# An inner seven-product scheme in one block product of the SwiGLU pairs

## The chip, the cores and the metric

The kernel runs on one core of one Trainium2 chip. The metric is the device time of one execution in microseconds. TensorE (PE) multiplies, with weight loads (PEld) that overlap matmuls; VectorE (DVE), ScalarE (ACT) and GpSimd (POOL) compute on vectors; SyncE (SP) and ScalarE issue DMAs. PSUM has eight banks of 128 x 512 float32, which TensorE writes and VectorE and ScalarE read.

## The reference, cut to what matters

One layer over 1024 positions and 1024 channels, all in float32: a modulated RMSNorm, a mixer (gated DeltaNet and short convolution) and its output projection, a second modulated norm, SwiGLU, and a final norm. The change lies in the SwiGLU:

```python
def swiglu(h, w_gate, w_up, w_down):
    return (jax.nn.silu(h @ w_gate) * (h @ w_up)) @ w_down
```

Here `h` is 1024 x 1024, `w_gate` and `w_up` are 1024 x 2816 (22 column tiles of 128), and `w_down` is 2816 x 1024.

## The kernel before, in words

**Precision.** A float32 operand is split into a high part (`hi`, rounded to float32r by ScalarE: `cast`, `split`) and a low part (the rest, subtracted by VectorE: `low`). A product takes three matmuls: hi x hi, hi x lo, lo x hi.

**Pairs and steps.** The products `h @ w_gate` and `h @ w_up` go over eleven pairs of column tiles (`p` = 0 to 10). For a pair, weights and `h` are cut into 2 x 2 blocks (by column tile and by half of the 1024 channels; by half of the channels and by half of the positions), and seven block products take the place of eight. `STEPS` names them in order: a PSUM bank pair (X, Y or Z), a weight block or sum of blocks (A11, A12, S2, S1, S3, S4, A22) and a block or sum of `h` (B11, B21, T2, T1, T3, B22, T4). `run(p, s)` issues step `s`: for gate (`q` = 0) and up (`q` = 1), four channel tiles `k` with three matmuls of 512 columns each, 24 in all. Step 1 is Y = A12 x B21. X collects four steps, Z two; in between, ScalarE copies X or Z out (`keep`), and VectorE adds what comes later (`close`). SiLU (`silu`, ScalarE) and the product with the up half (`act`, VectorE) follow.

**What sets the order.** In this stage no scheduler moves anything: each engine runs its instructions in the order in which the code issues them. `block(p, s)`, issued behind `run(p, s)`, holds what VectorE and ScalarE do beside the next steps: closing sums, weight sums of the pair (`sum_n`), casts and lows for later steps, those of A11 and A12 for the next pair (in blocks 5 and 6), the sums of the finished blocks that the down projection needs, and at `s == 0` the SiLU of bank X of the pair before and its product. DMAs wait in a list (`store`) until `flush` puts them on SP's queue; the weights of the next pair are loaded there at steps 3 and 5, into a buffer whose old blocks must have been read.

**Banks and buffers.** Bank X of pair p and Y of pair p + 1 are the same two banks (`bk`), so step 1 of a pair can write only when the SiLU and the product on X of the pair before have read. Split weights lie in eight buffers (`slot`): four in the ring `hl` and four under the tag `gl`; pair 0 uses `hl` alone.

**Ahead of the pairs.** While TensorE does the last tiles of the output projection (`w_out_tile`), the normed positions are transposed into `H[k]` (`first_half`): `H[0]` to `H[3]` hold B11 and `H[4]` to `H[7]` B21, each a split tile of 128 channels x 512 positions. `sums_x` makes the sums T1 to T4 by position.

Lines: the recording layer issues everything ahead of this stage from line 450, TensorE issues here from line 88, the others from line 89.

## Time and profile before

| | |
|---|---|
| time, median of 3 runs (lowest, highest) | 1170.82 us (1170.2, 1170.95) |
| the profiled execution: time, span | 1169.63 us, 1167.8 us |
| granted TensorE clock | 0.999 |
| TensorE busy | 1157.2 us (99%) |
| weight loads busy | 968.1 us (83%) |
| VectorE, ScalarE busy | 920.7 us (79%), 546.1 us (47%) |
| matmuls | 5582, each with a weight load |
| pair 0 begins, pair 1 begins, the pairs end | 522.9, 570.6, 951.4 us |

Times in rows are microseconds from the start of the span. A row of a timeline gives start, duration, engine, line, operation, tiles (written <- read) and count, and in brackets the idle time ahead of it with what ended it. A row of a group gives busy time and mean duration in ns, then the idle time ahead. The end of a matmul is modelled, so the price of one is read from the distance of starts. PE's busy time counts matmuls that wait in the pipeline.

### The profile page before, as it was taken

To read this page: it belongs to the slowest core of one execution; us is meant where nothing else is said; L and a number is where in the kernel's file an instruction comes from. 1 tells how busy PE (TensorE), PEld (TensorE's weight loads), DVE (VectorE), ACT (ScalarE), POOL (GpSimd) and SP (SyncE) were. 2 spreads that over 40 slices of the span, in tenths; PEclk is the share of its full clock that TensorE was granted. 3 is DMA by queue.
4 is the path that set the end of the run, shared out by engine and by line. 5 is a ranking of instruction groups with operands and counts; after the bars stand their busy time and mean duration, and the time that the engine had idled before them with its cause. 6 is when DMAs were issued, how large, how long until landed. Compare 5 with 4: busy or idle time off the path is not lost.

```text
span 1167.8 us, 16456 instructions
## 1 busy us (share of the span) xinstructions
PE 1157.2 (99%) x5582; PEld 968.1 (83%) x5582; DVE 920.7 (79%) x1702; ACT 546.1 (47%) x1182; POOL 59.6 (5%) x100
## 2 busy tenths in 40 slices
PE   9999999999999999999999999999999999999997
PEld 7888888888888888888888888888888888888886
DVE  7898988898987898669776777776777687788676
ACT  6779733458634552325433333333333365443343
POOL 1110101001101010200000000000000000000002
PEclk9999999999999999999999999999999999999999
DMA  9633455534325555434264456446554589869413
GB/s 363 246 99 110 118 171 163 168 114 137 113 66 163 163 193 175 174 101 144 80 216 158 140 201 223 159 132 222 191 184 137 194 306 393 308 203 340 144 37 145
DMA packets 126453, 207.06 MB, mean 177 GB/s; under 512 B 20513, under 2 KB 45089, under 8 KB 126369
## 3 DMA queue, kind: packets, MB, share of 16 engines
q1 hardware_dynamic: 121520, 202.86, 51.5%
q10 hardware_dynamic: 4848, 3.15, 0.9%
q8 instruction: 44, 0.72, 0.3%
q14 instruction: 41, 0.33, 0.1%
HBM read 150.91 MB, written 55.05 MB: 176 GB/s over the span
## 4 chain that ended last, share of the span: by engine, by line
PE 93%; DVE 3%; ACT 2%; DMA 1%; issue 1%; SPq 0%; ACTq 0%; DVEq 0%
PE acc L88 35%; PE acc L450 24%; PE dn L88 17%; PE o L88 4%; PE o L450 4%; PE A L450 1%; PE K L450 1%; DMA wr<-in_w_in_dram 1%; DVE xo L89 1%; PE ab L450 1%; PE w L450 1%; PE u L450 1%; PE O L450 1%; PE tr L450 1%; PE kk L450 1%
## 5 line engine op out<-in xcount | busy, mean ns | idle before, releaser
L450 PE MATMUL acc<-h,u 128*128 128x512 f32 x1200 | 301.0, 398 | 0.0
L450 PEld LDWEIGHTS acc<-h,u 128*128 128x128 f32 x1200 | 219.0, 188 | 41.1
L88 PE MATMUL acc<-h,hl 128*128 128x512 f32 x600 | 140.1, 390 | 0.0
L88 PEld LDWEIGHTS acc<-h,hl 128*128 128x128 f32 x600 | 112.4, 188 | 23.2
L88 PE MATMUL acc<-h,u 128*128 128x512 f32 x456 | 106.1, 389 | 0.0
L88 PE MATMUL acc<-T,hl 128*128 128x512 f32 x432 | 101.4, 390 | 0.4 <-ACT cc L89 0.4
L88 PEld LDWEIGHTS acc<-h,u 128*128 128x128 f32 x456 | 85.6, 188 | 17.7
L88 PEld LDWEIGHTS acc<-T,hl 128*128 128x128 f32 x432 | 80.9, 188 | 17.5 <-ACT cc L89 0.9
L88 PE MATMUL dn<-h,h 128*128 128x512 f32 x396 | 90.7, 389 | 0.0
L89 DVE TENSOR_TENSOR xo<-xo,dn 128x512 f32<-128x512 f32 x84 | 57.0, 683 | 42.3 <-PE dn L88 34.8
L89 ACT COPY cc<-acc 128x512 f32<-128x512 f32 x66 | 38.4, 590 | 108.3 <-PE acc L88 108.3
L88 PEld LDWEIGHTS dn<-h,h 128*128 128x128 f32 x396 | 74.3, 188 | 15.4
L88 PE MATMUL acc<-T,u 128*128 128x512 f32 x360 | 84.0, 389 | 0.0
L88 PEld LDWEIGHTS acc<-T,u 128*128 128x128 f32 x360 | 67.6, 188 | 14.0
L450 ACT CAST u<-raw 128x512 fp32r<-128x512 f32 x69 | 42.7, 622 | 66.0 <-PE acc L450 64.3
L89 DVE TENSOR_TENSOR cc<-cc,acc 128x512 f32<-128x512 f32 x66 | 43.8, 682 | 29.8 <-PE acc L88 29.8
L89 DVE TENSOR_TENSOR hl<-R,hl 128x512 fp32r<-128x512 f32 x60 | 39.4, 687 | 33.5 <-ACT hl L89 33.4
L450 DVE TENSOR_TENSOR u<-raw,u 128x512 fp32r<-128x512 f32 x82 | 56.0, 685 | 11.9 <-ACT u L450 11.7
L450 DVE SCALAR_TENSOR_TENSOR cv<-pr,cols_a,cv 128x512 f32<-128x512 f32 x72 | 52.9, 745 | 0.1
L89 ACT CAST h<-rw 128x512 fp32r<-128x512 f32 x57 | 32.7, 618 | 40.5 <-PE dn L88 34.6
L89 ACT CAST hl<-R 128x512 fp32r<-128x512 f32 x60 | 35.7, 622 | 23.5 <-DVE R L89 10.7
L89 DVE TENSOR_TENSOR u<-R,u 128x512 fp32r<-128x512 f32 x46 | 30.1, 686 | 20.6 <-ACT u L89 20.5
(343 smaller groups left out, 1993.2 us busy)
## 6 DMA issues: line engine op xcount, KB each, us to landing
raw<-in_w_in_dram SPq DMA_DIRECT2D x82, 256.0 KB, 3.1
am_scr<-cc SPq DMA_DIRECT2D x77, 256.0 KB, 4.6
raw<-in_w_ada_dram SPq DMA_DIRECT2D x56, 256.0 KB, 3.4
rw<-am_scr SPq DMA_DIRECT2D x55, 256.0 KB, 5.2
rw<-bm_scr SPq DMA_DIRECT2D x53, 256.0 KB, 5.3
bm_scr<-raw SPq DMA_DIRECT2D x51, 256.0 KB, 5.4
R<-in_w_gate_dram SPq DMA_DIRECT2D x22, 512.0 KB, 4.3
R<-in_w_up_dram SPq DMA_DIRECT2D x22, 512.0 KB, 5.5
```

What stands on the lines that cost most here:

```text
L88: return call(*a, **k)
L89: ins = call(*a, **k)
L450: ins = call(*a, **k)
```

## The change

Step 1 of pairs 1 to 10 is itself computed by seven products instead of eight. A12 (128 gate columns and 128 up columns, 512 channels) is cut by gate and up and by halves of the channels; B21 by halves of the channels and of the positions. Each of the products m1 to m7 has two channel tiles of three matmuls with 256 columns: 42 matmuls in place of 24 with 512.

The weight side needs three sums of blocks, in four operands of VectorE: `inner_sums` (four sums of 256 columns), and split weights I0 to I3 (`inner_cast`, `inner_low`: three of 512 columns and one of 256, where A12 had two of 512). The side of `h` needs q1, q2 and q3, made once in `inner_half`, which takes the place of `first_half(range(4, 8))`, and a fourth sum, which `inner_last` writes over the second half of `H[4]` and `H[5]` behind step 6 of pair 0. Pair 0 keeps the old step 1.

The seven products share two banks: x (m1, m6, m7, m4) in the bank that the SiLU frees, y (m2) and z (m5, m3) in the two halves of the other. Between products that add to one bank, ScalarE copies the sum so far (K0 behind m1, K2 behind m5, K1 behind m6, K3 behind m7), and `close_inner` adds copies and banks. m7 and m4 stand behind the two halves of step 2. The copy of X (`keep`) is issued ahead of the inner products, and in block 0 the product on X and its store stand ahead of S1 and S2. The scratch space for DMA descriptors is set to 1024 bytes.

```diff
+    def inner_half(a):
+        DVE.tensor_tensor(db3[:, a:a + 1], b2c[:, 6 + a:7 + a], b2c[:, 4 + a:5 + a], ALU.subtract)
+        bank = {}
+        for k in (4 + a, 6 + a):
+            bank[k] = allb.get("tr")
+            H[k][0] = tr_split(lambda: h_slot(k, 0), [x2n[i][:, k * P:(k + 1) * P] for i in range(4)], bank[k], b2c[:, k:k + 1])
+        pa, pb = bank[4 + a], bank[6 + a]
...
+        DVE.tensor_copy(f3, pa[:, HN:HT])
+        DVE.tensor_tensor(f1, f3, pa[:, 0:HN], ALU.subtract)
+        DVE.tensor_tensor(f2, pb[:, HN:HT], f1, ALU.subtract)
+        DVE.tensor_tensor(f3, pb[:, HN:HT], f3, ALU.subtract)
+        for n, f, col in (("q1", f1, None), ("q2", f2, b2c[:, 6 + a:7 + a]), ("q3", f3, db3[:, a:a + 1])):
+            hi, lo = tq[n][:, 0, a, :], tq[n][:, 1, a, :]
+            if col is None:
+                split(f, hi, lo, DVE)
+            else:
+                ACT.activation(hi, f, AF.Identity, bias=col, scale=1.0)
+                DVE.scalar_tensor_tensor(lo, f, col, hi.bitcast(F32), ALU.add, ALU.subtract)
+
+    def inner_last():
+        for a in (0, 1):
+            t = raw_t([P, 2, HN])
+            DVE.tensor_tensor(t, H[6 + a][0][:, :, 0:HN].bitcast(F32), tq["q2"][:, :, a, :].bitcast(F32), ALU.subtract)
+            DVE.tensor_tensor(t[:, 0], t[:, 0], t[:, 1], ALU.add)
+            q4 = H[4 + a][0][:, :, HN:HT]
+            split(t[:, 0], q4[:, 0], q4[:, 1], DVE)
...
-    first_half(range(4, 8))
+    inner_half(0)
+    inner_half(1)
...
+        def inner_sums(self):
+            g, u = self.m["A12"]
...
+            DVE.tensor_tensor(L[:, 0], u[:, 0:2], u[:, 2:4], ALU.add)
+            DVE.tensor_tensor(L[:, 1], L[:, 0], g[:, 0:2], ALU.subtract)
+            DVE.tensor_tensor(L[:, 3], g[:, 0:2], u[:, 0:2], ALU.subtract)
+            DVE.tensor_tensor(L[:, 2], g[:, 2:4], L[:, 1], ALU.subtract)
+            Lf = L.rearrange("p s k c -> p (s k) c")
+            self.iu = [None] * 4
+            self.src = [g, Lf[:, 0:4], Lf[:, 4:8], u[:, 2:4]]
...
-        n = n_slot[0] - 14
+        n = n_slot[0] - 12
...
+    INNER = {"m1": (0, 0, "x"), "m2": (0, 2, "y"), "m5": (1, 0, "z"), "m6": (1, 2, "x"), "m3": (2, 0, "z"), "m7": (2, 2, "x"), "m4": (3, 2, "x")}
...
+    def inner(p, ms):
...
+        for m in ms:
+            i, k0, d = INNER[m]
+            first = m in ("m1", "m2", "m5")
+            u = W[p].iu[i]
+            for k in range(2):
+                for n, (wi, xi) in enumerate(((0, 0), (0, 1), (1, 0))):
+                    pmm(iw[p][d], u[:, wi, k0 + k, :], inner_b(m, k, xi), first and k == 0 and n == 0, k == 1 and n == 2, not first)
+            if m in ("m1", "m5", "m6", "m7"):
...
+                ACT.copy(ik[p][:, {"m1": 0, "m6": 1, "m5": 2, "m7": 3}[m]], iw[p][d])
+
+    def close_inner(p, n):
+        (g, u), K, w = c[p][n], ik[p], iw[p]
+        DVE.tensor_tensor(g, g, flat(K[:, 0:2]), ALU.add)
+        DVE.tensor_tensor(u[:, HN:HT], u[:, HN:HT], K[:, 2], ALU.add)
+        DVE.tensor_tensor(g, g, w["yz"], ALU.add)
+        DVE.tensor_tensor(u[:, HN:HT], u[:, HN:HT], K[:, 3], ALU.add)
+        DVE.tensor_tensor(u[:, 0:HN], u[:, 0:HN], w["x"], ALU.add)
...
         elif s == 2:
-            close(p, "p1", "Y")
+            close_inner(p, "p1")
...
         elif s == 6:
             close(p, "u2", "Z")
             if n:
-                n.cast("A12", 0)
+                n.inner_sums()
+                n.inner_cast(0)
             silu(p, "u2")
             if n:
-                n.cast("A12", 1)
-                n.low("A12", 0)
-                n.low("A12", 1)
+                n.inner_cast(1)
+                n.inner_low(0)
+                n.inner_low(1)
...
+            if n:
+                for i in (2, 3):
+                    n.inner_cast(i)
+                    n.inner_low(i)
...
+        if s == 6:
+            inner_last()
...
-            run(p, s)
+            if s == 1:
+                keep(p, "p1", "X")
+                inner(p, ("m1", "m2", "m5", "m6", "m3"))
+            elif s == 2:
+                run(p, s, (0,))
+                inner(p, ("m7",))
+                run(p, s, (1,))
+                inner(p, ("m4",))
+            else:
+                run(p, s)
```

What this makes of the order on the engines is shown at three places.

TensorE, step 1 of pair 1 before: `acc_5922` and `acc_5923` are Y of gate and up, the `hl` tiles the split A12, the `h` tiles B21.

```order
L88 MATMUL acc_5922<-h_0_960_5218,hl_5862 128x512 x3
L88 MATMUL acc_5922<-h_0_962_5226,hl_5862 128x512 x3
L88 MATMUL acc_5922<-h_0_964_5234,hl_5862 128x512 x3
L88 MATMUL acc_5922<-h_0_966_5242,hl_5862 128x512 x3
L88 MATMUL acc_5923<-h_0_960_5218,hl_5865 128x512 x3
```

And now, from m1 to the first rows of step 2: `acc_5976` is bank x, `acc_5977` holds y and z, `u_5897`, `u_5900` and `u_5907` are I0, I1 and I2, the `q` tiles are q1 and q2.

```order
L88 MATMUL acc_5976<-h_0_960_5223,u_5897 128x256 x3
L88 MATMUL acc_5976<-h_0_966_5252,u_5897 128x256 x3
L88 MATMUL acc_5977<-h_0_962_5231,u_5897 128x256 x3
L88 MATMUL acc_5977<-h_0_968_5260,u_5897 128x256 x3
L88 MATMUL acc_5977<-q_5087,u_5900 128x256 x6
L88 MATMUL acc_5976<-q_5088,u_5900 128x256 x6
L88 MATMUL acc_5977<-h_0_962_5231,u_5907 128x256 x3
L88 MATMUL acc_5977<-h_0_968_5260,u_5907 128x256 x3
L88 MATMUL acc_5934<-T_1008_5536,hl_5966 128x512 x3
```

One wide product has become five narrow ones ahead of step 2; m6 returns to the bank of m1, and m3 to the bank of m5.

ScalarE between pair 0 and the first steps of pair 1, before: `cc_5787<-acc_5451` is the SiLU on bank X of pair 0, `S_5912` is S2, `acc_5883` and `acc_5884` are X of pair 1 and `S_5910` is S1.

```order
L89 ACTIVATE cc_5748<-cc_5748 128x512
L89 CAST hl_5865<-R_5745 128x512
L89 ACTIVATE cc_5787<-acc_5451 128x512
L89 CAST u_5914<-S_5912 128x512
L89 CAST u_5916<-S_5912 128x512
L89 COPY cc_5948<-acc_5883 128x512
L89 COPY cc_5948<-acc_5884 128x512
L89 CAST u_5951<-S_5910 128x512
```

The same place now; `L_5892` are the sums of `inner_sums`, `raw_5913` and `raw_5918` those of `inner_last`, `L_5984` the copies K.

```order
L89 ACTIVATE cc_5778<-cc_5778 128x512
L89 CAST u_5900<-L_5892 128x512
L89 CAST u_5907<-L_5892 128x512
L89 CAST u_5910<-R_5775 128x256
L89 CAST h_0_960_5223<-raw_5913 128x256
L89 CAST h_0_966_5252<-raw_5918 128x256
L89 ACTIVATE cc_5817<-acc_5481 128x512
L89 CAST hl_5966<-S_5964 128x512
L89 CAST hl_5968<-S_5964 128x512
L89 COPY cc_5973<-acc_5934 128x512
L89 COPY cc_5973<-acc_5935 128x512
L89 COPY L_5984<-acc_5976 128x256
```

The SiLU on X now stands behind the casts of `inner_last`, and the first copy K0 behind the casts of S2 and the copies of X.

VectorE from the first of the two sums behind the product of pair 0 (`cc_5526`) to the sum S1 (`S_5962`), now; before, these two sums were followed at once by S1.

```order
L89 TENSOR_TENSOR cc_5526<-cc_5778,cc_5817 128x512
L89 TENSOR_TENSOR cc_5778<-cc_5525,cc_5778 128x512
L89 TENSOR_TENSOR u_5907<-L_5892,u_5907 128x512
L89 TENSOR_TENSOR u_5910<-R_5775,u_5910 128x256
L89 TENSOR_TENSOR raw_5913<-h_0_962_5231,q_5088 128x512
L89 TENSOR_TENSOR raw_5913<-raw_5913 128x256
L89 TENSOR_TENSOR h_0_960_5223<-raw_5913,h_0_960_5223 128x256
L89 TENSOR_TENSOR raw_5918<-h_0_968_5260,q_5088 128x512
L89 TENSOR_TENSOR raw_5918<-raw_5918 128x256
L89 TENSOR_TENSOR h_0_966_5252<-raw_5918,h_0_966_5252 128x256
L89 TENSOR_TENSOR cc_5817<-acc_5482,cc_5817 128x512
L89 TENSOR_TENSOR S_5962<-R_5772,R_5775 128x1024
```

Two lows, six instructions of `inner_last` and the product on X have come in ahead of S1.

More of the change, by code (lines that the diff above doesn't have):

```diff
@@ L546 @@
     db2 = cst.tile([P, 4], F32, name="db2", tag="db2")
+    db3 = cst.tile([P, 2], F32, name="db3", tag="db3")
     su = []
@@ L1558, in first_half @@
             H[k][0] = tr_split(lambda: h_slot(k, 0), [x2n[i][:, k * P:(k + 1) * P] for i in range(4)], allb.get("tr"), b2c[:, k:k + 1])
+    HN = HT // 2
+    tq = {n: hp_.tile([P, 2, 2, HN], F32R, name=n, tag=n) for n in ("q1", "q2", "q3")}
+    def inner_half(a):
[5 more added lines that the diff above has]
+        pa, pb = bank[4 + a], bank[6 + a]
+        f12, f3 = raw_t(), raw_t()
+        f1, f2, f3 = f12[:, 0:HN], f12[:, HN:HT], f3[:, 0:HN]
+        DVE.tensor_copy(f3, pa[:, HN:HT])
[16 more added lines that the diff above has]
+            split(t[:, 0], q4[:, 0], q4[:, 1], DVE)
     def w_out_tile(t, ch):
@@ L1690, in mat, with inner_cast, inner_low @@
                 self.low(n, q)
+        def inner_sums(self):
+            g, u = self.m["A12"]
+            L = self.L = mp.tile([P, 4, 2, P], F32, name=nm("L"), tag="L", bufs=1)
+            DVE.tensor_tensor(L[:, 0], u[:, 0:2], u[:, 2:4], ALU.add)
[5 more added lines that the diff above has]
+            self.src = [g, Lf[:, 0:4], Lf[:, 4:8], u[:, 2:4]]
+        def inner_cast(self, i):
+            u = self.iu[i] = slot()
+            ACT.copy(u[:, 0] if i < 3 else u[:, 0, 2:4], self.src[i])
+        def inner_low(self, i):
+            u = self.iu[i]
+            hi, lo = (u[:, 0], u[:, 1]) if i < 3 else (u[:, 0, 2:4], u[:, 1, 2:4])
+            DVE.tensor_tensor(lo, self.src[i], hi.bitcast(F32), ALU.subtract)
     n_slot = [0]
@@ L1734, in run, with inner_b @@
                     pmm(ps, u[:, wi, k, :], x_[:, xi, :], first and k == 0 and n == 0, k == 3 and n == 2, not first)
+    iw, ik = {}, {}
+    INNER = {"m1": (0, 0, "x"), "m2": (0, 2, "y"), "m5": (1, 0, "z"), "m6": (1, 2, "x"), "m3": (2, 0, "z"), "m7": (2, 2, "x"), "m4": (3, 2, "x")}
+    def inner_b(m, k, xi):
+        if m in ("m1", "m4"):
+            return H[4 + k][0][:, xi, 0:HN] if m == "m1" else H[4 + k][0][:, xi, HN:HT]
+        if m in ("m2", "m3"):
+            return H[6 + k][0][:, xi, 0:HN] if m == "m2" else H[6 + k][0][:, xi, HN:HT]
+        return tq[{"m5": "q1", "m6": "q2", "m7": "q3"}[m]][:, xi, k, :]
+    def inner(p, ms):
+        if p not in iw:
+            x_, yz = bank_tile(bk[p][0]["Y"], "acc"), bank_tile(bk[p][1]["Y"], "acc")
+            iw[p] = dict(yz=yz, y=yz[:, 0:HN], z=yz[:, HN:HT], x=x_[:, 0:HN])
+        for m in ms:
[6 more added lines that the diff above has]
+            if m in ("m1", "m5", "m6", "m7"):
+                if p not in ik:
+                    ik[p] = mp.tile([P, 4, HN], F32, name=nm("L"), tag="L", bufs=1)
+                ACT.copy(ik[p][:, {"m1": 0, "m6": 1, "m5": 2, "m7": 3}[m]], iw[p][d])
[6 more added lines that the diff above has]
+        DVE.tensor_tensor(u[:, 0:HN], u[:, 0:HN], w["x"], ALU.add)
     def cc(p, n):
@@ L1800, in block @@
                 o = p - 1
-                ACT.activation(c[o]["z5"][1], bk[o][0]["X"], AF.Silu)
+                a12 = c[o]["z5"][1]
+                ACT.activation(a12, bk[o][0]["X"], AF.Silu)
+                DVE.tensor_tensor(a12, bk[o][1]["X"], a12, ALU.mult)
+                store(o, "A12", a12)
             if w:
@@ L1806, in block @@
                     w.cast("S2", q)
-            if p > 0:
-                a12 = c[o]["z5"][1]
-                DVE.tensor_tensor(a12, bk[o][1]["X"], a12, ALU.mult)
-                store(o, "A12", a12)
             if w:
@@ L1815, in block @@
             if w:
-                keep(p, "p1", "X")
+                if not p:
+                    keep(p, "p1", "X")
                 w.cast("S1", 0)
@@ L1973 @@
                 flush()
-            run(p, s)
+            if s == 1:
+                keep(p, "p1", "X")
+                inner(p, ("m1", "m2", "m5", "m6", "m3"))
[6 more added lines that the diff above has]
+                run(p, s)
             block(p, s)
@@ L2175 @@
     from concourse.bass_utils import run_bass_kernel_spmd as _run
-    nc = _bacc.Bacc("TRN2", target_bir_lowering=False, num_devices=1)
+    nc = _bacc.Bacc("TRN2", target_bir_lowering=False, num_devices=1, dynamic_dma_scratch_size=1024)
     arrays, args = {}, []
```

## The prediction

> **What bounds the kernel now.** I read the page first, then the waits of TensorE, then its timeline. The page:

> ```profile
> span 1167.8 us, 16456 instructions
> PE 1157.2 (99%) x5582; PEld 968.1 (83%) x5582; DVE 920.7 (79%) x1702; ACT 546.1 (47%) x1182; POOL 59.6 (5%) x100
> ...
> PE 93%; DVE 3%; ACT 2%; DMA 1%; issue 1%; SPq 0%; ACTq 0%; DVEq 0%
> ```

> TensorE is busy for 99% of the span, and 93% of the chain that ended last is its own work. Between 430 and 1000 us the waits of TensorE are one line, and the window of all eleven pairs shows the same:

> ```profile
> PE acc L88 <- ACT cc L89: 0.4, 1, 0.4
> ```

> ```profile
> 523.00:951.00 428.00, 427.56 (x1928) 354.91 (x1927) 313.76 (x464) 161.39 (x290) 0.76 (x2) 1.00 0.51 173
> ```

> In 428.00 us TensorE is idle for 0.44 us, at the full granted clock (1.00). So in the pairs a matmul saved is time saved, and every wait that the change brings to TensorE is time lost; nothing absorbs it. VectorE and ScalarE are off the path while their results come early enough. The timeline of TensorE gives the price of a wide matmul (512 columns):

> ```profile
> 570.63 11.04 PE L88 MATMUL acc<-h,hl 128*128 128x512 f32 x48
> 581.51 5.60 PE L88 MATMUL acc<-T,u 128*128 128x512 f32 x24
> ...
> 646.79 11.04 PE L88 MATMUL acc<-h,u 128*128 128x512 f32 x48
> ```

> Steps 0 and 1 of pair 1 run from 570.63 to 581.51, 48 matmuls in 10.88 us: 0.2267 us each, 5.44 us a step. Step 0 of pair 3 begins at 646.79.

> **The price of a narrow matmul.** The change puts 42 matmuls of 256 columns in the place of 24 of 512, each with its own weight load as before. No row has 256 columns. The nearest below:

> ```profile
> 239.77 1.06 PE L450 MATMUL K<-A,kt 128*128 128x128 f32 x8
> 240.58 0.70 PE L450 MATMUL acc<-h,u 128*128 128x512 f32 x2
> 241.12 1.05 PE L450 MATMUL O<-A,at 128*128 128x128 f32 x8
> ```

> From 239.77 to 241.12 stand eight matmuls of 128 columns and two wide ones: (1.35 - 2 x 0.2267) / 8 = 0.112 us. A quarter of the columns costs half the time, so there something else sets the pace, and what both sizes share is one weight load each. So 256 columns cost at least 0.112 us, about half a wide one (0.1133) if the columns set the pace and nothing is fixed, and 0.150 us if a straight line joins the two rows. I take 0.120: both limits that I can name lie at 0.112 to 0.113, and 7 ns are for what of a wide interval doesn't halve with its columns. Then step 1 costs 42 x 0.120 = 5.04 us instead of 5.44: 0.40 us saved in each of ten pairs (0.74 at 0.112; 0.86 lost at 0.150).

> A load's own record is longer than the narrow interval, so loads overlap what runs ahead of them:

> ```profile
> L450 PEld LDWEIGHTS K<-A,kt 128*128 128x128 f32 x120 | 15.5, 191 | 1.9 <-DVE A L450 0.5 <-issue 0.2
> ```

> [...]

> **Rows for the other engines.** Groups by form, busy time and mean ns behind the bar:

> ```profile
> L89 ACT COPY cc<-acc 128x512 f32<-128x512 f32 x66 | 38.4, 590 | 108.3 <-PE acc L88 108.3
> ...
> L89 DVE TENSOR_TENSOR cc<-cc,acc 128x512 f32<-128x512 f32 x66 | 43.8, 682 | 29.8 <-PE acc L88 29.8
> ```

> ```profile
> L450 DVE SCALAR_TENSOR_TENSOR S<-S,egl,K 128x128 f32<-128x128 f32 x56 | 15.7, 340 | 1.3 <-PE K L450 1.2
> L89 DVE TENSOR_TENSOR S<-S,R 128x1024 f32<-128x1024 f32 x10 | 12.2, 1225 | 0.3
> ```

> ```profile
> L450 ACT COPY S<-K x4: 265/279/300, 212.4 to 212.9; 128x128 f32<-128x128 f32 x4
> ```

> So 256 columns cost VectorE between 0.34 and 0.68 us, about 0.42, or some 0.34 in a row of independent ones (wide ones start 0.60 apart), and ScalarE between 0.28 and 0.59, about 0.38.

> **Pair 1: the wait that the change adds.** VectorE and ScalarE between pair 0 and pair 1:

> ```profile
> 567.30 1.28 DVE L89 TENSOR_TENSOR cc<-cc,acc 128x512 f32<-128x512 f32 x2
> 568.81 0.69 DVE L89 TENSOR_TENSOR hl<-R,hl 128x512 fp32r<-128x512 f32 x1 [0.23 <-ACT hl L89]
> 571.53 0.69 DVE L89 TENSOR_TENSOR hl<-R,hl 128x512 fp32r<-128x512 f32 x1 [2.03 <-ACT hl L89]
> ...
> 572.86 1.29 DVE L89 TENSOR_TENSOR cc<-cc,cc 128x512 f32<-128x512 f32 x2
> 574.07 1.22 DVE L89 TENSOR_TENSOR S<-R,R 128x1024 f32<-128x1024 f32 x1
> ...
> 576.46 0.68 DVE L89 TENSOR_TENSOR cc<-acc,cc 128x512 f32<-128x512 f32 x1
> ```

> ```profile
> 571.40 0.59 ACT L89 ACTIVATE cc<-acc 128x512 f32<-128x512 f32 x1
> 576.58 1.14 ACT L89 CAST u<-S 128x512 fp32r<-128x512 f32 x2 [4.58 <-DVE S L89]
> 577.63 1.07 ACT L89 COPY cc<-acc 128x512 f32<-128x512 f32 x2
> ```

> In the changed order VectorE does this from 568.5 on: the four sums of `inner_sums` (two wait for the one before them: 1.45), two lows (1.2; the weight buffers are others now, so the two waits for `hl` go), product and two sums (1.9), two more lows (0.95): 574.0. Then `inner_last`, twice a wide sum (0.68), a narrow one (0.45), a hand-over and a narrow cast on ScalarE (0.49), a narrow low (0.35), the last low beside what follows: ScalarE's second cast ends near 577.65. Behind it in ScalarE's queue stands the SiLU on bank X of pair 0, at 571.40 before and now ending at 578.25. It frees the bank that m1 writes, and m1 is due at 570.63 + 5.44 = 576.07: TensorE waits 2.2 us. From there VectorE needs 0.6 for the product that frees the other bank (in time for m2) and 2.5 for S1 and S2 (the rows' 574.07 to 576.46): 581.35. ScalarE then casts S2 (1.1), keeps X (1.05) and only then copies m1 out of its bank (0.4): 583.95. m6 adds to that bank and must wait for the copy. m1, m2 and m5 end at 578.25 + 18 x 0.12 = 580.4, so TensorE waits 3.55 us more. With m6 and m3 (1.44) step 2 starts at 585.4 where it started at 581.51: 3.9 us late, and m7 and m4 inside it add 1.44. Pair 1 costs 5.3 us more than before. By 583.4 both S2 lows are done, so no further wait follows. If the chain is shorter by 1 us, so is the loss.

> **Pairs 2 to 10: what the new work hides behind.** Each period gives VectorE some 3.5 us more (sums 1.45, lows 0.95, closing sums 2.3 instead of 1.2) and ScalarE four copies of 0.38 and 1.0 of casts. VectorE's waits in one period:

> ```profile
> 641.55 0.69 DVE L89 TENSOR_TENSOR cc<-cc,acc 128x512 f32<-128x512 f32 x1 [2.04 <-PE acc L88]
> ...
> 653.57 1.29 DVE L89 TENSOR_TENSOR hl<-S,hl 128x512 fp32r<-128x512 f32 x2 [2.44 <-ACT hl L89]
> ...
> 657.87 0.69 DVE L89 TENSOR_TENSOR cc<-cc,acc 128x512 f32<-128x512 f32 x1 [1.28 <-PE acc L88]
> ```

> ```profile
> 664.45 1.29 DVE L89 TENSOR_TENSOR u<-R,u 128x512 fp32r<-128x512 f32 x2 [2.95 <-ACT u L89]
> ...
> 669.89 1.29 DVE L89 TENSOR_TENSOR hl<-R,hl 128x512 fp32r<-128x512 f32 x2 [1.74 <-ACT hl L89]
> ```

> That is 10.4 us of cover. Walked from 641.55 as above, without `inner_last`: the last low of A12 ends at 647.8, S2 is split by 652.8 (due 655.8, step 2), S1 by 657.6 (due 662.7), the close ends at 663.4 instead of 658.6, S3 by 664.6 (due 668.2), S4 by 668.4 (due 673.6), A22 by 672.0 (due 679.0), and VectorE is back at its wait for step 5 with about 1.1 of the 2.04 us left. Two loads on SP's queue move:

> ```profile
> 671.22 0.37 SPq L89 DMA_DIRECT2D R<-in_w_gate_dram  x1
> ```

> ```profile
> R<-in_w_up_dram SPq DMA_DIRECT2D x22, 512.0 KB, 5.5
> ```

> The second half of the next weights waits for A22's low and goes out 0.7 us later than at 671.22; it lands near 677.9, and `inner_sums` wants it at 679.6. The first half waits for S3's low, 4.8 us later, and is needed 11 us on. The stores queued behind both have no reader in this stage; the store of A12 comes earlier. The one tight place is m3, which adds to the bank that ScalarE copies after m5. The kept X bank shows the delay:

> ```profile
> 652.43 0.59 ACT L89 COPY cc<-acc 128x512 f32<-128x512 f32 x1 [2.13 <-PE acc L88]
> ```

> The half ends at 652.23, the copy starts 0.20 later; with 0.38 for the copy and about 0.05 back to TensorE that is 0.63 us behind m5, and m6 covers 6 x 0.12 = 0.72. I cost it at 0.03 us a pair, 0.3 in all; without the cover (a copy as long as a wide one) it is 0.12 a pair, 1.1.

> **The transition before pair 0.** `inner_half` gives VectorE 5.7 us more at 496 us (per half four sums 1.75, three lows 1.15). Behind it VectorE waits for TensorE at

> ```profile
> 500.79 0.69 DVE L89 TENSOR_TENSOR x<-x,o 128x512 f32<-128x512 f32 x1 [0.24 <-PE o L88]
> ...
> 506.37 0.69 DVE L89 TENSOR_TENSOR x<-x,o 128x512 f32<-128x512 f32 x1 [0.97 <-PE o L88]
> ...
> 511.94 0.69 DVE L89 TENSOR_TENSOR x<-x,o 128x512 f32<-128x512 f32 x1 [2.36 <-PE o L88]
> ...
> 517.51 0.69 DVE L89 TENSOR_TENSOR x<-x,o 128x512 f32<-128x512 f32 x1 [0.99 <-PE o L88]
> ```

> These take up 4.6 us of it; the walk from row to row leaves 0.8 us at 523, ahead of the splits of pair 0. There the cover is thin: the low of S2 that step 2 needs ends at 535.74, and the step starts 1.5 us later.

> ```profile
> 535.06 0.68 DVE L89 TENSOR_TENSOR hl<-S,hl 128x512 fp32r<-128x512 f32 x1
> ```

> ```profile
> 537.24 3.01 PE L88 MATMUL acc<-T,hl 128*128 128x512 f32 x12
> ```

> Some of the transposes behind it wait for banks with less, and the one wait of TensorE in the pairs (0.4 us, above) stands in this stretch too. I take 0.4, between 0 and 1.1.

> **The sum.** Nine pairs save 9 x 0.40 = 3.6; pair 1 loses 5.3; the m3 places 0.3; the transition 0.4: 2.4 us more. Against the profiled execution (1169.63 us, 1.83 of it outside its span) that is 1172.0; the median of the three runs is 1.19 us above that execution, 1170.82, so I forecast 1173.2. A difference of 0.2% (2.3 us) is about what a measurement of this kernel can tell from none; the forecast stands at that edge.

> **Rivals.**
> - *The narrow matmuls run at the limit of their loads* (0.112): the other side. Nine pairs save 9 x 0.74 = 6.6, pair 1 loses 3.8 + 1.3 = 5.1, with 0.7 for the rest: 0.8 us less, 1170.0. The total crosses zero at 0.114 us, which is the point from which this decides. For it speaks the row at 0.112; against it, that it leaves nothing fixed in the wide interval, half of which is 0.1133 already. Chance 0.30. [...]
> - *The copies out of the banks hold TensorE in every pair*: m6 or m3 waits 0.3 to 0.5 us in nine pairs, 1176 to 1178. For it: the margin at m3 is 0.09 us. Against it: m6's copy has 0.8. Chance 0.13.
> - *The straight line holds* (0.150): nine pairs lose 7.7, pair 1 loses 6.0: 1185. Against it: what sets 0.112 is the load, which the columns of a longer matmul hide. Chance 0.03. [...]
> - *The wait in pair 1 isn't there*, because the sums behind pair 0 run faster than walked or the casts change places: 1168 or a little under. Against it: the order of both queues; for it, that the walk adds some twenty durations, most of them bounded and not read. Chance 0.12.

> The forecast itself gets 0.42, of which a little over half lies above the edge. Slower: 0.24 + 0.13 + 0.03, and 0.03 of the loads' limit with a longer wait = 0.43; same: 0.18, 0.18 of the loads' limit = 0.36; faster: 0.12, 0.09 of the loads' limit with a wait shorter by 1.5 us or more = 0.21. The range goes from 1167.5 (the rival without the wait, with 0.5 us for its little under) to 1178 (the copies' rival).

> **What would show it.** In the profile after: 128x256 matmuls starting 0.120 us apart (42 of them and 24 wide ones in 10.48 us); TensorE's waits with a first one for ScalarE at pair 1, near 2.2 us, and a second before m6, near 3.5, with ScalarE's SiLU on X near 577.7; the later pairs 37.68 us apart instead of 38.08, with no wait over 0.1 us. I am wrong if the pairs' period is not below 38.0, if pair 1 shows less than 4 us of waits, or if a wait returns in every pair.

## The result: slower by 0.42%, with two waits in pair 1 and half the granted clock behind them

The changed kernel takes 1175.57 us (median; 1172.99 to 1176.67) against 1170.26 before: ratio 1.0042, 95% interval 1.0029 to 1.0055. The forecast was 1173.2, slower by 2.4 us; measured are 5.3. The profiled execution took 1172.99 us, the lowest of its runs. Its page:

```profile
span 1171.2 us, 17025 instructions
...
PE 1156.9 (99%) x5762; PEld 974.5 (83%) x5762; DVE 960.9 (82%) x1814; ACT 569.3 (49%) x1250; POOL 60.1 (5%) x100
```

There are 180 matmuls more, TensorE's busy time is 0.3 us less, and the span is 3.4 us longer. The window of the eleven pairs:

```profile
524.12:954.78 430.66, 426.37 (x2110) 361.56 (x2108) 349.62 (x561) 182.26 (x352) 0.76 (x2) 1.00 0.51 172
```

Where 0.44 us of the pairs were idle, 4.29 are (430.66 - 426.37). Of TensorE's waits between 430 and 1010 us, one of the two in the first line and the one in the second are new:

```profile
PE acc L88 <- ACT cc L89: 2.4, 2, 1.9
PE acc L88 <- ACT L L89: 1.9, 1, 1.9
```

TensorE's timeline shows both in pair 1, and pairs 2 and 3 without any:

```profile
571.97 5.60 PE L88 MATMUL acc<-h,hl 128*128 128x512 f32 x24
579.46 2.35 PE L88 MATMUL acc<-h,u 128*128 128x256 f32 x12 [1.89 <-ACT cc L89]
...
584.99 0.98 PE L88 MATMUL acc<-q,u 128*128 128x256 f32 x6 [1.90 <-ACT L L89]
...
620.68 1.60 PE L88 MATMUL acc<-h,u 128*128 128x256 f32 x12
622.11 1.60 PE L88 MATMUL acc<-q,u 128*128 128x256 f32 x12
623.55 0.88 PE L88 MATMUL acc<-h,u 128*128 128x256 f32 x6
624.27 2.90 PE L88 MATMUL acc<-T,hl 128*128 128x512 f32 x12
...
658.41 1.59 PE L88 MATMUL acc<-h,u 128*128 128x256 f32 x12
```

From 620.68 to 658.41 is one period, 37.73 us instead of 38.08. Its 30 narrow matmuls from 620.68 to 624.27 take 0.1197 us each, without a hole ahead of m6 (m5 and m6 are the row of q with x12) or ahead of m3 (the row behind it). ScalarE's timeline shows what pair 1 waits for:

```profile
578.51 0.41 ACT L89 CAST h<-raw 128x256 fp32r<-128x256 f32 x1 [1.56 <-DVE raw L89]
578.82 0.59 ACT L89 ACTIVATE cc<-acc 128x512 f32<-128x512 f32 x1
582.56 1.14 ACT L89 CAST hl<-S 128x512 fp32r<-128x512 f32 x2 [3.15 <-DVE S L89]
583.60 1.06 ACT L89 COPY cc<-acc 128x512 f32<-128x512 f32 x2
584.56 0.66 ACT L89 COPY L<-acc 128x256 f32<-128x256 f32 x2
```

The SiLU on X stands behind the second cast of `inner_last` and ends at 579.4; m1 starts at 579.46. K0 and K2 (the row of two copies to `L`) stand behind the casts of S2 and the copies of X; m6 starts at 584.99.

By stretches, in us, from the starts of matmuls (matmul 500 lies ahead of all that the change moves; the second profile is that of `after_again`, below):

| stretch | before | changed | changed, second profile | forecast of the difference |
|---|---|---|---|---|
| start to matmul 500 | 103.31 | 104.38 | 103.69 | 0 |
| matmul 500 to pair 1 | 467.32 | 467.59 | 468.31 | +0.4 |
| pair 1 | 38.08 | 43.27 | 45.82 | +5.3 |
| pairs 2 to 10 | 342.72 | 339.54 | 339.54 | -3.3 |
| time of that execution | 1169.63 | 1172.99 | 1175.55 | +2.4 |

The first profile has 1.07 us more at the start; without that it is 2.3 us over before, the forecast's 2.4. The second profile's time is that of the median; what it has beyond the first lies in pair 1 (2.55 us) and in the stretch ahead of it (0.72).

### The profile page after: what moved, and what is told of

Read it like the earlier page. It is cut to its first block, busy times and chain, and to the rows that moved or that the text cites. A ratio compares the mean times of both kernels' runs of the same rounds, so it can differ in the third digit from the quotient of the medians.

```text
span 1171.2 us, 17025 instructions
## 1 busy us (share of the span) xinstructions
PE 1156.9 (99%) x5762; PEld 974.5 (83%) x5762; DVE 960.9 (82%) x1814; ACT 569.3 (49%) x1250; POOL 60.1 (5%) x100
## 4 chain that ended last, share of the span: by engine, by line
PE 50%; DVE 4%; ACT 1%; issue 1%; POOL 0%; ACTq 0%; DVEq 0%; POOLq 0%
PE acc L88 32%; PE dn L88 17%; DVE xo L89 1%; DVE cc L89 0%; DVE T L89 0%; DVE S L89 0%; DVE hl L89 0%; DVE h L89 0%; ACT hl L89 0%; DVE x L89 0%; DVE raw L89 0%; ACT h L89 0%; ACT cc L89 0%; DVE u L89 0%; ACT jf L89 0%
## 5 line engine op out<-in xcount | busy, mean ns | idle before, releaser
L450 PE MATMUL acc<-h,u 128*128 128x512 f32 x1200 | 301.2, 398 | 0.0
L450 PEld LDWEIGHTS acc<-h,u 128*128 128x128 f32 x1200 | 219.0, 188 | 41.3
L88 PE MATMUL acc<-h,hl 128*128 128x512 f32 x576 | 135.2, 390 | 0.0
L88 PE MATMUL acc<-T,hl 128*128 128x512 f32 x552 | 131.5, 390 | 0.5 <-ACT cc L89 0.5
L88 PEld LDWEIGHTS acc<-h,hl 128*128 128x128 f32 x576 | 107.3, 188 | 21.8
L88 PEld LDWEIGHTS acc<-T,hl 128*128 128x128 f32 x552 | 102.1, 188 | 21.1 <-ACT cc L89 0.9
L88 PE MATMUL acc<-h,u 128*128 128x256 f32 (+1 forms) x480 | 90.3, 338 | 1.9 <-ACT cc L89 1.9
L89 DVE TENSOR_TENSOR xo<-xo,dn 128x512 f32<-128x512 f32 x84 | 57.0, 684 | 42.0 <-PE dn L88 34.7
L88 PE MATMUL dn<-h,h 128*128 128x512 f32 x396 | 90.7, 389 | 0.0
L88 PEld LDWEIGHTS acc<-h,u 128*128 128x128 f32 x480 | 77.4, 190 | 13.2 <-ACT cc L89 2.3
L88 PEld LDWEIGHTS dn<-h,h 128*128 128x128 f32 x396 | 74.3, 188 | 15.4
L450 ACT CAST u<-raw 128x512 fp32r<-128x512 f32 x69 | 42.7, 622 | 65.6 <-PE acc L450 64.9
L89 DVE TENSOR_TENSOR cc<-cc,acc 128x512 f32<-128x512 f32 x66 | 41.2, 641 | 33.4 <-PE acc L88 33.4
L450 DVE TENSOR_TENSOR u<-raw,u 128x512 fp32r<-128x512 f32 x82 | 56.2, 688 | 11.9 <-ACT u L450 11.6
L88 PE MATMUL acc<-T,u 128*128 128x512 f32 x240 | 56.0, 389 | 0.0
L89 ACT CAST hl<-S 128x512 fp32r<-128x512 f32 x44 | 25.2, 621 | 59.4 <-DVE S L89 59.4
L450 DVE SCALAR_TENSOR_TENSOR cv<-pr,cols_a,cv 128x512 f32<-128x512 f32 x72 | 52.9, 745 | 0.1
L88 PEld LDWEIGHTS acc<-T,u 128*128 128x128 f32 x240 | 45.0, 188 | 9.4
L89 ACT CAST h<-rw 128x512 fp32r<-128x512 f32 x57 | 32.7, 617 | 40.7 <-PE dn L88 34.6
L89 ACT ACTIVATE cc<-cc 128x512 f32<-128x512 f32 x33 | 20.9, 632 | 64.8 <-DVE cc L89 64.8
L89 DVE TENSOR_TENSOR hl<-S,hl 128x512 fp32r<-128x512 f32 x44 | 28.5, 687 | 28.0 <-ACT hl L89 28.0
L89 ACT CAST u<-R 128x512 fp32r<-128x512 f32 (+1 forms) x60 | 33.9, 581 | 35.2 <-DVE R L89 35.2
## 6 DMA issues: line engine op xcount, KB each, us to landing
R<-in_w_gate_dram SPq DMA_DIRECT2D x22, 512.0 KB, 3.9
R<-in_w_up_dram SPq DMA_DIRECT2D x22, 512.0 KB, 5.3
```

The source lines that it names most:

```text
L88: return call(*a, **k)
L89: ins = call(*a, **k)
L450: ins = call(*a, **k)
```

## Experiments

Each time stands beside the kernel before on the same chip: 1170.30 us with `after_again`, `before_scratch`, `last_late` and `copy_first`; 1170.67 with `after_heat`, `best`, `m3_first` and `halves`; 1170.56 with `best_again`, `best_loads` and `before_loads`.

**The changed kernel once more** (`after_again`, no edit).

> The changed kernel unedited, once more. In its profile the first matmuls of the execution lay 1.0 us later than before (four wide matmuls took 3.38 us instead of 2.44), ahead of all that the change touches, and the other runs lay up to 3.7 us above the profiled one. If that late start is chance, some profile of this kernel or of the kernel before will show it and others not, and the median lies 3 to 5 us above before. If it belongs to the changed program, this profile shows it again: matmul number 500 near 104.4 us, not 103.3. Pair 1 again 5.2 us longer than 38.08, the other pairs 37.73.

1175.55 us, ratio 1.0045 (1.0033 to 1.0058). Matmul 500 stood at 103.69, so the late start is chance. Pair 1 took 2.55 us more than in the first profile, where I had expected the same. The windows around its waits, first of the changed kernel, then of this one (the number ahead of the last two is the granted clock):

```profile
577.00:580.00 3.00, 1.11 (x7) 0.69 (x6) 2.42 (x5) 0.90 (x2) 0.00 (x0) 1.00 0.44 145
580.50:582.50 2.00, 2.00 (x11) 2.00 (x11) 1.97 (x2) 0.00 (x0) 0.00 (x0) 0.50 0.87 332
586.00:590.00 4.00, 4.00 (x25) 3.51 (x25) 3.06 (x5) 1.41 (x3) 0.00 (x0) 1.00 0.34 128
```

```profile
580.50:582.50 2.00, 2.00 (x11) 2.00 (x11) 1.97 (x2) 0.00 (x0) 0.00 (x0) 0.50 0.89 339
586.00:590.00 4.00, 4.00 (x16) 3.52 (x15) 2.36 (x4) 1.41 (x3) 0.00 (x0) 0.50 0.35 130
591.00:594.00 3.00, 3.00 (x18) 2.58 (x17) 1.03 (x3) 1.21 (x3) 0.00 (x0) 1.00 0.00 0
```

Behind the first wait the granted clock falls to 0.50 in both. In the first profile it is back at 1.00 when the second wait ends, so the half clock fell into time in which TensorE had to wait for K0 anyway; in the second it lasts until 590.7, and the matmuls from m3 on pay for it. The first half of step 2 there, against 2.90 in pair 2 above:

```profile
587.76 4.29 PE L88 MATMUL acc<-T,hl 128*128 128x512 f32 x12
```

The hole ahead of m1 in the first profile is 2.05 us (579.46 less 571.97 + 5.44). Its half clock begins at 580.25 and lasts 3.41 us; in the 3.41 us ahead of that TensorE was busy for 1.52 (the windows under `copy_first`, below).

**The scratch space alone** (`before_scratch`), in the kernel before:

```diff
-    nc = _bacc.Bacc("TRN2", target_bir_lowering=False, num_devices=1)
+    nc = _bacc.Bacc("TRN2", target_bir_lowering=False, num_devices=1, dynamic_dma_scratch_size=1024)
```

> The kernel before with nothing but the scratch space for DMA descriptors set to 1024 bytes, as the change sets it. Theory: the space costs nothing, since no instruction moves; same as before within 0.5 us, matmul number 500 near 103.3 us. Rival: the space is what makes the start 1.0 us later (and the runs spread by more): 1 to 2 us slower than before, matmul number 500 near 104.4 us.

1170.76 us, ratio 1.0005 (0.9996 to 1.0013): it costs nothing that can be measured. Matmul 500 stood at 104.06 us here and at 103.2 to 104.4 in the other profiles, with and without the change.

**The last operand sums later** (`last_late`). `inner_last` gets one scratch tile, taken where it stood, and is issued in pair 1 ahead of step 2:

```diff
         if s == 6:
-            inner_last()
+            q4_raw = raw_t([P, 2, HN])
...
                 inner(p, ("m1", "m2", "m5", "m6", "m3"))
+                if p == 1:
+                    inner_last(q4_raw)
```

> The last operand sums move from behind step 6 of pair 0 to behind the inner products ahead of step 2 of pair 1, on VectorE and on ScalarE; m4, which reads them, comes 5 us later. Theory (the queue order makes pair 1 wait): the SiLU on bank X is done near 572.5 us, so the wait at m1 (2.05 us) and the one at m2 (0.7) go; S1 and S2 come 4 us earlier, but so do m1 to m5, and m6 still waits some 1.9 us for K0 behind the casts of S2 and the copies of X: 3 to 4 us less than the changed kernel. Rival (the sums cost VectorE time that has to be paid anyway): the wait moves to step 2, 3 or m4 of pair 1, under 1.5 us less.

1169.68 us, ratio 0.9997 (0.9988 to 1.0006), 5.9 us under the changed kernel beside it. TensorE in pair 1:

```profile
577.65 1.59 PE L88 MATMUL acc<-h,u 128*128 128x256 f32 x12
579.08 0.88 PE L88 MATMUL acc<-q,u 128*128 128x256 f32 x6
581.16 0.98 PE L88 MATMUL acc<-q,u 128*128 128x256 f32 x6 [1.20 <-ACT L L89]
```

The wait at m1 is gone; that at m6 is left, 1.2 us where I expected 1.9, and behind it narrow matmuls start 0.12 apart: the clock did not fall behind this hole (it was 1.00 from 580.5 to 582.5 us). Pair 1 takes 39.19 us: 4.08 less than in the first profile of the changed kernel, where the half clock cost nothing, and 6.63 less than in the second, where it did. So the saving of the medians exceeds the expected 3 to 4 us by about what the half clock costs.

**K0 ahead of the copies of X** (`copy_first`), in every pair:

```diff
+                inner(p, ("m1",))
                 keep(p, "p1", "X")
-                inner(p, ("m1", "m2", "m5", "m6", "m3"))
+                inner(p, ("m2", "m5", "m6", "m3"))
```

> In each pair ScalarE's copy K0 of m1 is issued ahead of the copies of X instead of behind them; all else as in the changed kernel. Theory: K0 stands behind the casts of S2 alone, so m6 of pair 1 begins 0.95 us earlier and the other pairs, which have 0.8 us to spare there, stay: 0.9 to 1.0 us less than the changed kernel. Rival (what holds m6 is the time of the copy and the way from bank to bank, not the queue): no change, or a new wait at step 2 for the copies of X.

1174.06 us, 1.5 under the changed kernel beside it, but the intervals overlap (1.0022 to 1.0049). The profile decides: m6 starts 4.55 us behind m1 instead of 5.53, 0.98 less as expected, and m3 now waits for K2 behind the copies of X:

```profile
581.83 1.71 PE L88 MATMUL acc<-h,u 128*128 128x256 f32 x12 [1.90 <-ACT cc L89]
...
586.38 0.98 PE L88 MATMUL acc<-q,u 128*128 128x256 f32 x6 [2.13 <-ACT L L89]
587.63 1.65 PE L88 MATMUL acc<-h,u 128*128 128x256 f32 x6 [0.27 <-ACT L L89]
```

The half clock came behind the second hole here (six narrow matmuls of m3 in 1.45 us), not behind the first, though that is 2.06 us long as well. The granted clock changes at 580.25 and 583.66 us in the first profile of the changed kernel, at 580.44 and 590.68 in the second, at 587.60 and 591.02 here: the half clock lasted 3.41, 10.24 and 3.42 us. Windows of 3.4 us that end at a fall, or lie ahead of one, first of the changed kernel, then of this one:

```profile
576.83:580.24 3.41, 1.52 (x10) 1.05 (x9) 2.68 (x6) 1.02 (x3) 0.00 (x0) 1.00 0.46 156
```

```profile
577.37:580.77 3.40, 2.56 (x12) 1.79 (x10) 2.86 (x7) 0.41 (x1) 0.00 (x0) 1.00 0.00 1
580.78:584.18 3.40, 2.35 (x18) 2.22 (x18) 2.83 (x5) 0.90 (x2) 0.00 (x0) 1.00 0.93 337
584.20:587.60 3.40, 1.04 (x7) 0.78 (x6) 2.68 (x5) 2.68 (x7) 0.00 (x0) 1.00 0.12 45
```

In the windows that end at a fall TensorE was busy for 1.52 us (changed kernel) and 1.04 (here); in the two ahead of the latter, over which the first hole here is split, for 2.56 and 2.35. So the length of a hole alone did not tell whether the clock fell behind it. What does, no run isolates; nor is it shown why the two profiles of the changed kernel, with the same holes, have 3.41 and 10.24 us of half clock.

**TensorE kept busy in the waits of the changed kernel** (`after_heat`; `heat1(n)` issues n wide matmuls into a bank that nobody reads; pair 1 alone):

```diff
...
+                    keep(p, "p1", "X")
+                    heat1(8)
+                    inner(p, ("m1", "m2", "m5"))
+                    heat1(13)
+                    inner(p, ("m6", "m3"))
...
```

> The changed kernel with idle TensorE kept busy in pair 1: 8 wide matmuls into a free bank ahead of m1 and 13 ahead of m6, whose results nobody reads. They take 1.8 and 2.95 us, less than the idle times there. Theory: in most executions the two waits make the chip halve TensorE's clock for 3.4 to 10 us behind them (narrow matmuls 0.213 us apart instead of 0.119, wide ones 0.427 instead of 0.227, in the second profile of the changed kernel up to 590.7 us), and this, not the waits' length, is what its median has over its first profiled run. With TensorE kept busy the waits end where they ended, no interval of 0.213 or 0.427 is left, and the median falls by 2 to 3 us, to about 1173, with less spread. Rival (the slow stretch has another cause, such as contention for a bank or a memory port): the intervals and the median stay.

1174.03 us, ratio 1.0032 (1.0020 to 1.0044): 3.4 us over before instead of 5.3. The windows:

```profile
580.50:582.50 2.00, 2.00 (x19) 1.96 (x18) 1.97 (x3) 0.00 (x0) 0.00 (x0) 1.00 1.04 397
586.00:590.00 4.00, 4.00 (x25) 3.51 (x24) 2.91 (x5) 1.41 (x3) 0.00 (x0) 1.00 0.35 131
```

The clock stays at 1.00, and pair 1 takes 43.26 us, as in the first profile of the changed kernel. So the half clock went with the idle time: filled with work of no use, the same waits had none behind them in this profile. The size is less sure: 1.9 us in the medians is under the 2 to 3 expected, and the intervals overlap.

**Both waits removed** (`best`). To the late sums comes, in pair 1 alone, the order K0, casts of S2, K2, copies of X, K1 (block 0 of pair 1 leaves out S2's casts and lows):

```diff
+                if p == 1:
+                    inner(p, ("m1",))
+                    for q in (0, 1):
+                        W[p].cast("S2", q)
+                    for q in (0, 1):
+                        W[p].low("S2", q)
+                    inner(p, ("m2", "m5"))
+                    keep(p, "p1", "X")
+                    inner(p, ("m6", "m3"))
...
```

> The late last operand sums, and in pair 1 alone ScalarE's queue in the order K0, casts of S2, K2, copies of X, K1; the lows of S2 go with the casts. Theory: the 1.2 us that m6 waits in the kernel with the late sums goes, since K0 is done 0.6 us behind m1; no wait over 0.3 us is left in pair 1, its period is near 37.9 us, and the time is 1.2 us under that kernel and 1.8 under before, 1168.5. Rival (S2's casts, 0.3 us later, or the sums pushed behind them are due next): a wait of 0.3 to 1 us at step 2, at m4 or at step 3, and nothing gained.

1168.62 us, ratio 0.9983 (0.9974 to 0.9992). Pair 1 takes 37.73 us, like the others:

```profile
578.47 1.60 PE L88 MATMUL acc<-h,u 128*128 128x256 f32 x12
579.90 1.60 PE L88 MATMUL acc<-q,u 128*128 128x256 f32 x12
581.34 0.88 PE L88 MATMUL acc<-h,u 128*128 128x256 f32 x6
582.06 2.90 PE L88 MATMUL acc<-T,hl 128*128 128x512 f32 x12
```

> The kernel with the pair 1 order once more, on the chip on which the early loads are tried: 1.5 to 2.5 us under before, stretch to pair 1 between 467.6 and 470 us, pairs 1 to 10 at 37.73 us each.

The same kernel on another chip (`best_again`): 1169.05 us, ratio 0.9984 (0.9975 to 0.9992), 1.5 us under before. Its pairs take 37.75 us; the stretch to pair 1, 466.9 us, lies under the range that I gave.

**The copies without their cover** (`m3_first`): m3 ahead of m6 in the changed kernel.

> The changed kernel with m3 ahead of m6, so that nothing covers ScalarE's copy K2 of the bank to which m3 adds. Theory: m3 waits 0.55 to 0.6 us in each of nine pairs (m5's end to the copy's end, 622.83 to 623.40 us in the changed kernel), and 0.3 in pair 1: 5 to 5.7 us more than the changed kernel; holes so short don't lower the clock. Rival (the copies are no constraint of that size): under 1 us more.

1183.38 us, ratio 1.0106 (1.0092 to 1.0119): 12.7 us over before against 5.3 of the changed kernel, so 7.4 more where I expected 5 to 5.7. Each later pair takes 38.46 us, 0.73 more, at the full clock; pair 1 has two stretches of 3.41 us at half clock (granted were 0.64 in 580.5 to 582.5 us and 0.73 in 586 to 590). A later pair:

```profile
702.10 0.88 PE L88 MATMUL acc<-q,u 128*128 128x256 f32 x6
703.45 0.98 PE L88 MATMUL acc<-h,u 128*128 128x256 f32 x6 [0.46 <-ACT L L89]
```

m3 starts 1.35 us behind m5 instead of 0.72: 0.63 of wait, the figure of the prediction. Another 0.10 goes behind the hole, where the first narrow matmul takes 0.222 us.

**The width alone** (`halves`): in the kernel before, step 1 as 48 matmuls of 256 columns (two halves of the positions, all eight products).

> The kernel before with step 1 of pairs 1 to 10 as 48 matmuls of 256 columns in place of 24 of 512: same sums, eight products, no copies, no sums added. Theory: a narrow matmul costs 0.1195 us by itself, 48 of them 5.74 us instead of 5.44: 0.30 a pair, 3.0 us slower than before. Rival (the 0.1195 of the changed kernel is helped or hurt by its copies and bank halves): under 1.5 us slower if the price is 0.1133 to 0.115 here, over 4 if it is above 0.122.

1173.15 us, ratio 1.0025 (1.0016 to 1.0034): 2.5 us slower where I expected 3.0. Pairs take 38.42 us, 0.34 more than before: 48 x 0.12 - 5.44 = 0.32. The narrow price is the same without the copies and the added sums.

**The early loads** (`best_loads`, `before_loads`). In three of the eight profiles that have the change and these loads on ScalarE (`copy_first`, `after_heat`, `best`), pair 0 was late too. VectorE ahead of it in the kernel with both waits removed:

```profile
519.38 1.28 DVE L89 SCALAR_TENSOR_TENSOR x<-x,st,u 128x1024 f32<-128x1024 f32 x1 [4.39 <-DMA x_scr<-x]
```

ScalarE's queue there, and in the kernel before:

```profile
502.75 0.39 ACTq L89 DMA_DIRECT2D er<-in_w_gate_dram  x1
```

```profile
495.24 0.94 ACTq L89 DMA_DIRECT2D er<-in_w_gate_dram  x1
```

VectorE overwrites `x` and waits for its store; four loads for pair 0 have moved 7.5 us later on ScalarE's queue, behind `inner_half`, close ahead of the store before that one, at 507.00. The edit, in that kernel and in the one before:

```diff
-            ACT.dma_start(out=t, in_=src[n * HT:(n + 1) * HT, 0:P].rearrange("(kk p) c -> p kk c", p=P))
+            SP.dma_start(out=t, in_=src[n * HT:(n + 1) * HT, 0:P].rearrange("(kk p) c -> p kk c", p=P))
```

> The kernel with the pair 1 order (late sums, K0 first), and the four early loads of pair 0's weights issued by SyncE, which is idle there, instead of ScalarE. Theory: in the changed kernel these loads stand in ScalarE's queue behind inner_half's instructions and go out near 502.8 us, not 495.2; the store of x behind them then shares the DMA engines with them, and VectorE, which overwrites x, waits for it (3.0 and 4.4 us at 510 and 519 us where the kernel before waited 2.6), so that TensorE's transposes in pair 0 wait: matmul number 500 to the start of pair 1 was 467 to 469 us before and 467.6 to 470.5 with the change. With the loads off that queue that stretch is near 467.5 us in every profile and the time falls by 1 us against the same kernel without this, to about 1167.5. Rival (the lateness is inner_half's own VectorE work): no change.

> The kernel before with the same four loads issued by SyncE. Theory: there they went out at 495.2 us, early enough, and nothing waits for them; same as before within 0.5 us. Rival (loads on SyncE help any kernel of this kind, and what the other run gains is not the change's cost given back): over 0.7 us less.

With both waits removed and this edit: 1167.36 us, ratio 0.9973 (0.9964 to 0.9982), lowest to highest 1.3 us apart, where the same kernel without it had 5.1 beside it and 2.6 on the other chip. VectorE waits for no store any more:

```profile
517.82 1.28 DVE L89 SCALAR_TENSOR_TENSOR x<-x,st,u 128x1024 f32<-128x1024 f32 x1 [2.60 <-POOL st L89]
```

In the kernel before the edit does nothing: 1170.38 us, 0.9999 (0.9990 to 1.0008). So in the medians it gives back 1.7 us of a cost of the change, but the intervals with and without it still touch (0.9964 to 0.9982, 0.9975 to 0.9992), and the repeat without it was itself profiled with no wait for a store.

The long wait has a nearer cause than the four loads. Its store, in the kernel with both waits removed, went out behind a weight load of SP's queue:

```profile
514.76 0.38 SPq L89 DMA_DIRECT2D R<-in_w_gate_dram  x1
515.02 0.33 ACTq L89 DMA_DIRECT2D x_scr<-x  x1
```

It landed 4.2 us later. In the three profiles with a wait of 3.9 to 4.4 us this store was issued 0.17 to 0.26 us behind that load and took 3.8 to 4.2 us; in the other five, and with the edit, it was issued 0.02 to 0.12 us ahead of it and took 2.3 to 2.7; before, it was issued 1.9 us ahead and took 2.0. The store at 507.00, behind the four loads, is late as well: it lands in 2.7 to 2.8 us in these three profiles (2.2 to 2.5 in the other five, 2.0 before and with the edit), and VectorE, which waits for it too, comes 0.3 to 0.4 us later. That the order of these two DMAs makes the store slow is inferred from the profiles; no run changes it alone.

The stretch from matmul 500 to pair 1 doesn't show this cost cleanly: the scratch space alone, without the change, had 469.0 us there where the kernel before had 467.3. From matmul 2350 (440.68 us before, still ahead of the change) to pair 1 the profiles without the change have 129.9 to 130.5 us, the changed kernel 130.1 and 130.4, the three with the long wait 131.6 to 132.2. Of the two other late ones, the late sums (468.8 in the longer stretch) have 130.6 here and owe more than half of their delay to what stands ahead of the change; m3 ahead (469.2) has 131.1: VectorE waits 0.78 us there at 532.63 for a load of weights, where the changed kernel's profiles show no such wait. Why that load was late stays open.

## Why the prediction was right, and where it fell short

- **The narrow price**: forecast 0.120, measured 0.1197, in `halves` 0.120. The rivals at 0.112 and 0.150 are out. That the load sets 0.112 was my reading of one row; no run shows it, and loads' records in the changed kernel are 0.19 us long where matmuls start 0.120 apart. A period is 37.73, not 37.68: the first two wide matmuls behind narrow ones take 0.233 to 0.236 us.
- **Pair 1**: both waits at the places and in the order forecast, the first 2.05 us for 2.2, the second 3.37 for 3.55 (m1's 579.46 + 18 x 0.12 to m6's 584.99). The period grew by 5.19 us for 5.3. That the queue order makes them is shown by `last_late` and `best`, which change that order and lose first one wait, then both; the rival without a wait is out.
- **The step that failed** is the price of these waits: I wrote that a wait costs TensorE its own length. Behind the first one the granted clock also fell to 0.50, at no cost in the one profile and at 2.55 us in the other; `after_heat`, with the same waits and no idle TensorE, has no half clock. The profile of before, idle for 0.4 us at a time, could not show that.
- **The side work of pairs 2 to 10** hides as walked: I left about 1.1 of VectorE's 2.04 us ahead of step 5's close in pair 2, and the row has 1.05.

```profile
647.73 0.69 DVE L89 TENSOR_TENSOR cc<-cc,acc 128x512 f32<-128x512 f32 x1 [1.05 <-PE acc L88]
```

- **The copies**: forecast 0.3 us in all for m3, measured nothing. The margin behind m5 (0.63 of 0.72) was right, as `m3_first` shows; m6 covers it in full. The rival of a wait in every pair is out.
- **The transition**: forecast 0.4. From matmul 2350 to pair 1 the two profiles of the changed kernel are 0.2 and 0.4 us over before, and 0.5 is what the kernel with the scratch space alone has too: the term can't be told from chance there. My working of it has a slip (5.7 less 4.6 is 1.1, where I wrote 0.8). I walked VectorE and left out the DMAs that its work moves; in three other profiles that made 1.7 to 2.2 us.
- **Luck**: the forecast's 2.4 us agree with the fastest of six executions, whose half clock cost nothing; the median has 5.3. It lies within the range only because the upper end was set by the copies' rival, which the runs exclude, and not by anything that I knew of the clock.

## What to carry to other kernels

Price a one-time set-up step by the queues it lands in: sums issued ahead of a bank's release cost 4.1 us and more at the start of a scheme that gains 0.35 us a round; issued behind it, and with the copies in the order in which they are waited for, they cost nothing that shows in pair 1 (37.73 us like the others). Read the granted clock behind a hole on TensorE, and in more than one profile: behind the 2.05 us here it was 0.50, which cost nothing in one profile and 2.55 us in another. Between matmul groups that add to one bank, put a group as long as the copy needs: here 0.72 us of m6 covered 0.63, and without the cover a pair took 0.73 us more.
